# Differential attention: the low halves of the queries stored over all 128 partitions

## The chip, the cores and the metric

The kernel runs on one core of a Trainium2 chip. The metric is the device time of one execution in microseconds (us). TensorE (PE) multiplies matrices and transposes, VectorE (DVE) and ScalarE (ACT) do element-wise work, reductions and exponentials, GpSimd (POOL) does some of the casts and additions, and SyncE (SP) issues most transfers.

## The reference

The reference is a network of two layers over 512 latent and 256 context tokens of width 1024. Layer 0 mixes tokens with delta-rule and retention heads, layer 1 with differential softmax attention; each is followed by a layer norm, a gated feed-forward part with a 3x3 convolution, and another layer norm. Only layer 1's mixer matters here. It has 8 heads; each has two maps of queries and keys with 64 features and values with 128 features. The 512 latent queries read all 768 tokens:

```python
def diff_mix(q, k, v, lam):
    s = jnp.einsum('cbhqd,cbhkd->cbhqk', q, k).astype(jnp.float32) * DIFF_HD ** -0.5
    p = jax.nn.softmax(s, -1)
    a = p[0] - lam * p[1]
    return jnp.einsum('bhqk,bhkd->bhqd', a.astype(v.dtype), v)
...
    lp = lam_p.astype(f32)
    lam = jnp.exp(jnp.sum(lp[0] * lp[1])) - jnp.exp(jnp.sum(lp[2] * lp[3])) + lambda_init
```

After it come a root-mean-square norm per head and the output product with `w_out`. All is float32.

## The kernel before, in words

A float32 product is made of float32r (fp32r) products. Each operand is split into a high part (a rounding cast) and a low part (the rest), and three products are summed: high by high, high by low, low by high. Weights come in units: `unit` loads one (`raw`), ScalarE casts its high part `whi` (L147), and VectorE or GpSimd subtracts for the low part `wlo` (L148).

The program is written with a framework that orders the instructions of each engine by a priority, which is the place in the code plus an offset (`self.priority`). Each engine then runs its list in that fixed order and waits on semaphores.

`odd_mixer` (L1539) is the mixer of layer 1. It works on pairs of heads. `project` makes q, k and v of one pair, by pairs of token tiles: products `opj` of 256 columns (L115), the axial rotation `rope` (VectorE multiplies into `otok` and `ob`, L1574 and L1578; GpSimd adds, L1580), four transposes into `oT_ps` (L119), and then the evacuation with the split:

- `q_evac` (L1584) writes three tiles: the high part of map 0 on both halves of the partitions, the high part of map 1 likewise, and one tile with the low part of map 0 on partitions 0 to 63 and that of map 1 on 64 to 127. These are four ScalarE casts and two VectorE subtractions.
- `k_evac` writes for map 0 the high part on the lower and the low part on the upper partitions, and for map 1 the other way round.

`attend` handles one head, by four query tiles of 128 queries; 8 heads make 32 tiles. Per tile and map it fills a PSUM tile `sc` of 768 scores, by a piece of 512 and one of 256 columns. One product over all 128 rows gives high by high plus high by low (the query's high part is there twice). Two further products, over 64 rows each, add low by high. So a tile has four products over 128 rows and four over 64:

```python
for k0, n in ((0, 512), (512, 256)):
    for c, rows in enumerate((LO, HI)):
        self.mm(scs[c][:, k0:k0 + n], q[2][rows, i, t * P:(t + 1) * P], k[c][rows, i, k0:k0 + n],
                start=False)
```

Then VectorE takes the maximum `mx` (L1664) and scales it (L1665), ScalarE takes exponentials `pt` with their sum (L1667), VectorE forms the factor `nl` (L1671, L1672) and combines the two maps (L1675), TensorE transposes the result in six pieces (`aT_ps`, L119), ScalarE and VectorE copy them (L1683), and TensorE multiplies by the values (L115). VectorE copies the result into `oall` (L1687).

While heads of one pair are attended, the projection products of the next pair are emitted as filler, three steps per query tile, with a priority 100 later; so the scheduler puts `opj` products among the score products wherever these would wait. For the last pair the filler is the output product (`wo_ps`). The pools of the first steps, the constants `ca`, `sub`, `lp` and `nlam` among them, are opened before; `lp` and `l2` hold lambda's products.

Of the kernel before, what the change touches and what calls it, by code (L numbers as in the profile page):

```python
# [11 lines left out]
F32 = mybir.dt.float32  # L12
F32R = mybir.dt.float32r
I32 = mybir.dt.int32
AF = mybir.ActivationFunctionType
ALU = mybir.AluOpType
AX = mybir.AxisListType
# [3 lines left out]
P = 128  # L21
# [76 lines left out]
class Net:  # L98
# [22 lines left out]
    def rsqrt(self, pool, x, n, mul, add, tag):  # L121
        """(x*mul + add)^-0.5 on [128, n] float32, by three Newton steps (each flips the sign) to full precision."""
# [27 lines left out]
    def pin(self, ins):  # L150
        """Queue an instruction behind all that its engine was given so far."""
        return self.tc.keep_in_program_order(ins)

    @contextmanager
    def priority(self, offset):
        """Emit with a priority shifted by offset (positive: later)."""
# [9 lines left out]
    def hilo(self):  # L166
        """The two split halves of the next weight unit, from the open weight pools in turn."""
# [6 lines left out]
    def unit(self, parts, scale=None):  # L174
        """Load weight columns (list of [1024, w] DRAM blocks), scaled if asked for, and split them: [128, 8, 256]."""
# [14 lines left out]
    def unit_rows(self, src, scale=None):  # L190
        """Load [256, 1024] weight rows, with columns scaled if given, and split them: [128, 2, 1024]."""
# [10 lines left out]
    def proj_fm_g(self, w, c0, dsts):  # L202
        """Feature-major products: dsts = [(psum [128, n], t0, n)]; weights stationary."""
# [9 lines left out]
    def proj_tm_g(self, ps, w, t, c0=0, n=256):  # L213
        """Token-major products for token tile t; activations stationary."""
# [19 lines left out]
    def set_work(self, items, side=None):  # L234
        """items: [(weight parts, generator function of the loaded unit)], run in order by tick()."""
# [13 lines left out]
    def _step(self):  # L249
        """Advance the current item; its cost, or None at its end."""  # L250
# [19 lines left out]
    def drain(self, upto):  # L270
        """Run until the first `upto` items are complete."""
# [4 lines left out]
    def setup(self):  # L276
# [22 lines left out]
        self.cpad = cp.tile([P, KT, 32], F32, name="cpad")  # L299
        nc.gpsimd.memset(self.cpad, 0.0)  # L300
# [10 lines left out]
    def rows_T(self, pool, psp, src, n, dst, doff=0):  # L311
        """DRAM rows [n, 128] -> dst[:, doff:doff+n] (transposed)."""
# [7 lines left out]
    def cond(self, pool, psp):  # L320
        """silu(c), silu(c_ctx) as a zero-padded stationary operand [128, 8, 32]."""
# [22 lines left out]
    def mod_bias(self, pool, psp, l):  # L344
        """mod_b of layer l, per feature: [128, 48]."""
# [8 lines left out]
    def mod_group_g(self, mp, psp, l, g, tag="tr", bufs=2):  # L354
        """adaLN columns [2048 g, 2048 (g+1)) of layer l, both conditionings."""
# [30 lines left out]
    def h_params(self, key, lnidx, l, sub):  # L386
        """Scale/bias per feature of h = modulate(layer_norm(.)): from xhat."""
# [1426 lines left out]
```

## Time and profile before

| | us |
|---|---|
| runs | 2127.46, 2130.88, 2131.03 |
| median | 2130.88 |
| span of the profiled execution | 2123.7 |
| TensorE busy | 1976.3 (93%) |
| VectorE busy | 1297.5 (61%) |
| GpSimd busy | 789.0 (37%) |
| ScalarE busy | 703.5 (33%) |
| mean granted clock of TensorE | 0.971 |

The profile gives the profiled execution a span, from its first to its last instruction, of 2123.7 us, and no other time of its own; the three runs were 3.8 to 7.3 us above that span. The attention lies at about 1333 to 1670 us. In the rows below a line such as `PE L115 MATMUL sc<-ok,oq 64*128 64x512` reads: TensorE, line 115, product into the tile `sc` from `ok` and `oq`, 64 rows by 128 columns of the array, 512 columns streamed; `x6` counts like instructions in a run. A duration of TensorE overlaps the next one; the distance between starts is what an instruction takes of the engine. What stands in brackets is the time that the engine was idle before, and what ended it.

### The profile page before, as it was taken

The page shows a single profiled execution, that of the slowest core. Times are in us where ns is not written, and L with a number is a line of the kernel's source. Part 1 is how long each engine was busy: PE and PEld are TensorE (multiplying, and loading weights), DVE is VectorE, ACT ScalarE, POOL GpSimd, SP SyncE. Part 2 cuts the span into 40 slices and gives each one's busy share as a digit, 9 for nine tenths or more (in the row PEclk, how much of TensorE's full clock was granted, in tenths as well). Part 3 has the DMA queues.
Part 4 walks back from the last instruction along what each step waited for, and adds up shares of the span by engine and source line. Part 5 has one row for each costly group of instructions (what it writes and reads, how often), then busy time and mean ns, then how long its engine had stood idle before and what let it go on. Part 6 is the DMA issues. An engine that isn't in the chain of part 4 may idle for free. (4 is left out here: it accounts for less than half of the span.)

```text
span 2123.7 us, 33676 instructions
## 1 busy us (share of the span) xinstructions
PE 1976.3 (93%) x13766; PEld 1676.6 (79%) x13766; DVE 1297.5 (61%) x2570; ACT 703.5 (33%) x1228; POOL 789.0 (37%) x430
## 2 busy tenths in 40 slices
PE   6989999999998999999999988988997989999997
PEld 4777777778898988888888868878886987777776
DVE  2354745544358675665555584566567787767676
ACT  2331343523344422222222243444444453222221
POOL 1233222212422344444444442212023135756582
PEclk8999999999999999999999999999997999999999
DMA  8536335465623311111111112100103142223221
GB/s 255 166 121 181 109 119 149 126 182 168 180 80 120 124 65 60 60 60 60 60 60 60 60 60 68 41 29 32 41 31 100 50 139 100 99 80 99 80 80 40
DMA packets 195586, 201.34 MB, mean 95 GB/s; under 512 B 21112, under 2 KB 183512, under 8 KB 195432
## 3 DMA queue, kind: packets, MB, share of 16 engines
q1 hardware_dynamic: 194136, 197.57, 29.2%
q8 instruction: 108, 1.77, 0.3%
q10 hardware_dynamic: 1296, 1.62, 0.3%
q14 instruction: 46, 0.38, 0.1%
HBM read 185.89 MB, written 13.27 MB: 94 GB/s over the span
## 5 line engine op out<-in xcount | busy, mean ns | idle before, releaser
L148 POOL TENSOR_TENSOR wlo<-raw,whi 128x2048 fp32r<-128x2048 f32 (+2 forms) x154 | 416.7, 2730 | 533.6 <-ACT whi L147 509.4
L1442 DVE SCALAR_TENSOR_TENSOR ac<-g_ps,fconvT,ac 128x441 f32<-128x441 f32 (+2 forms) x352 | 244.4, 694 | 190.9 <-ACT ac L1431 180.9
L147 ACT CAST whi<-raw 128x2048 fp32r<-128x2048 f32 (+2 forms) x177 | 200.4, 1169 | 393.5 <-PE d_ps L115 180.9
L115 PE MATMUL d_ps<-whi,hh 128*128 128x512 f32 x440 | 177.8, 404 | 21.1 <-DVE gt L1391 20.0
L115 PE MATMUL d_ps<-whi,hl 128*128 128x512 f32 x440 | 172.8, 393 | 0.6 <-DVE hl L148 0.6
L115 PE MATMUL d_ps<-wlo,hh 128*128 128x512 f32 x440 | 172.9, 393 | 0.0
L1488 POOL TENSOR_TENSOR acc<-acc,gt 128x512 f32<-128x512 f32 x90 | 129.7, 1450 | 69.4 <-DVE gt L1391 69.4
L115 PE MATMUL opj<-whi,hTh 128*128 128x256 f32 x512 | 151.6, 296 | 1.1 <-ACT oq L1591 1.1
L1391 DVE TENSOR_TENSOR gt<-d_ps,gate 128x512 f32<-128x512 f32 x192 | 130.6, 684 | 31.1 <-PE d_ps L115 28.9
L115 PE MATMUL opj<-whi,hTl 128*128 128x256 f32 x512 | 148.1, 289 | 0.0
L115 PE MATMUL opj<-wlo,hTh 128*128 128x256 f32 x512 | 147.9, 289 | 0.0
L115 PE MATMUL g_ps<-hTl,whi 128*128 128x512 f32 (+1 forms) x384 | 144.7, 377 | 1.1 <-POOL hTl L148 1.1
L115 PE MATMUL u_ps<-hTl,whi 128*128 128x512 f32 (+1 forms) x384 | 144.8, 377 | 0.2
L115 PE MATMUL u_ps<-hTh,wlo 128*128 128x512 f32 (+1 forms) x384 | 144.6, 377 | 0.0
L115 PE MATMUL u_ps<-hTh,whi 128*128 128x512 f32 (+1 forms) x384 | 144.5, 377 | 0.0
L115 PE MATMUL g_ps<-hTh,whi 128*128 128x512 f32 (+1 forms) x384 | 144.4, 376 | 0.0
L115 PE MATMUL g_ps<-hTh,wlo 128*128 128x512 f32 (+1 forms) x384 | 144.2, 376 | 0.0
L115 PE MATMUL fpj<-whi,hTh 128*128 128x256 f32 x432 | 126.9, 294 | 5.8 <-DVE kT L550 4.7
L115 PE MATMUL fpj<-wlo,hTh 128*128 128x256 f32 x432 | 126.9, 294 | 0.0
L115 PEld LDWEIGHTS d_ps<-whi,hh 128*128 128x128 f32 x440 | 83.0, 189 | 55.2 <-DVE gt L1391 38.9
L115 PE MATMUL fpj<-whi,hTl 128*128 128x256 f32 x432 | 126.0, 292 | 0.0
L115 PEld LDWEIGHTS opj<-whi,hTh 128*128 128x128 f32 x512 | 98.8, 193 | 7.2 <-issue 4.4
(464 smaller groups left out, 5014.8 us busy)
## 6 DMA issues: line engine op xcount, KB each, us to landing
mraw<-in_mod_w_dram SPq DMA_DIRECT2D x80, 512.0 KB
raw<-in_f_w_gate_dram SPq DMA_DIRECT2D x22, 1024.0 KB
raw<-in_f_w_up_dram SPq DMA_DIRECT2D x22, 1024.0 KB
raw<-in_f_w_down_dram SPq DMA_DIRECT2D x22, 1024.0 KB
raw<-in_o_w_qkv_dram SPq DMA_DIRECT2D x12, 1024.0 KB
raw<-in_e_w_in_dram SPq DMA_DIRECT2D x10, 1024.0 KB
mraw<-in_mod_w_dram SPq DMA_DIRECT2D x32, 256.0 KB
raw<-in_e_w_in_dram SPq DMA_DIRECT2D x12, 512.0 KB
```

The costliest lines, as they stand in the source:

```text
L115: self.nc.tensor.matmul(out, lhsT=lhsT, rhs=rhs, start=start, stop=stop)
L147: self.nc.scalar.copy(h, r)
L148: lo_eng.tensor_sub(l, r, h.bitcast(F32))
L1391: v.tensor_mul(gt, ps, gates[0 if t < NLT else 1][:, n * 512:(n + 1) * 512])
L1442: v.scalar_tensor_tensor(out=o, in0=pv[:, r0 + di:r1 + di, c0 + dj:c1 + dj], scalar=cw[(di + 1) * 3 + dj + 1], in1=o, op0=ALU.mult, op1=AL ...
L1488: (v if n else g).tensor_add(o, o, gt)
```

## The change

The low part of each map's query is stored over both halves of the partitions, as the high part is; there are four query tiles instead of three. Every score product then runs over 128 rows, and low by low is added to the sum. The products come map by map: high 512, high 256, low 512, low 256 of map 0, then of map 1. `q_evac` has six ScalarE casts (two of them copy the low part from the one half to the other) and two VectorE subtractions.

Three more edits free memory for the fourth tile: the zero pad `cpad` moves from the pool of constants into a pool of layer 0's mixer, `lp` and `l2` into a pool `olp` of their own that is closed at once, and the rotation's `ob` has one buffer instead of two. The other lines of the diff take comments out.

```diff
-        self.cpad = cp.tile([P, KT, 32], F32, name="cpad")
-        nc.gpsimd.memset(self.cpad, 0.0)
...
     def even_mixer(self, accst):
         w_in = self.a["e_w_in"][0]
         with ExitStack() as outer:
             with ExitStack() as right:
                 p2 = self.pool(right, "d2", bufs=2, side="right")
+                self.cpad = p2.tile([P, KT, 32], F32, bufs=1, name="cpad")
+                self.nc.gpsimd.memset(self.cpad, 0.0)
...
-                lp = cpl.tile([P, 4, DH], F32, name="lp")
-                nc.scalar.dma_start(out=lp, in_=a["o_lambda"][0].partition_broadcast(P))
-                l2 = cpl.tile([P, 2], F32, name="l2")
-                for i in range(2):
-                    v.tensor_mul(lp[:, 2 * i], lp[:, 2 * i], lp[:, 2 * i + 1])
-                    v.reduce_sum(l2[:, i:i + 1], lp[:, 2 * i], axis=AX.X)
-                s_.activation(l2, l2, AF.Exp)
                 nlam = cpl.tile([P, 1], F32, name="nlam")
-                v.tensor_sub(nlam, l2[:, 1:2], l2[:, 0:1])
-                v.tensor_scalar_add(nlam, nlam, -LAMBDA_INIT)
+                with ExitStack() as tmp:
+                    lpp = self.pool(tmp, "olp")
+                    lp = lpp.tile([P, 4, DH], F32, name="lp")
+                    nc.scalar.dma_start(out=lp, in_=a["o_lambda"][0].partition_broadcast(P))
+                    l2 = lpp.tile([P, 2], F32, name="l2")
+                    for i in range(2):
+                        v.tensor_mul(lp[:, 2 * i], lp[:, 2 * i], lp[:, 2 * i + 1])
+                        v.reduce_sum(l2[:, i:i + 1], lp[:, 2 * i], axis=AX.X)
+                    s_.activation(l2, l2, AF.Exp)
+                    v.tensor_sub(nlam, l2[:, 1:2], l2[:, 0:1])
+                    v.tensor_scalar_add(nlam, nlam, -LAMBDA_INIT)
 
                 def rope(ps, t, out):
                     pv, ov = (x.rearrange("p (t h f n) -> p t h f n", t=2, h=4, f=2) for x in (ps, out))
-                    b = p2.tile([P, 2, 4, 2, 32], F32, tag="ob", name="ob")
+                    b = p2.tile([P, 2, 4, 2, 32], F32, tag="ob", bufs=1, name="ob")
                     v.tensor_mul(out.rearrange("p (t x n) -> p t x n", t=2, n=32),
                                  ps.rearrange("p (t x n) -> p t x n", t=2, n=32),
                                  cos[:, t:t + 2].unsqueeze(2).to_broadcast([P, 2, 8, 32]))
...
                 LO, HI = slice(0, DH), slice(DH, P)
 
                 def q_evac(q, ps, cs):
-                    s_.copy(q[0][LO, :, cs], ps[LO])
-                    s_.copy(q[1][HI, :, cs], ps[HI])
-                    v.tensor_sub(q[2][LO, :, cs], ps[LO], q[0][LO, :, cs].bitcast(F32))
-                    v.tensor_sub(q[2][HI, :, cs], ps[HI], q[1][HI, :, cs].bitcast(F32))
-                    s_.copy(q[0][HI, :, cs], ps[LO])
-                    s_.copy(q[1][LO, :, cs], ps[HI])
+                    for c, src in enumerate((ps[LO], ps[HI])):
+                        own, other = (LO, HI) if c == 0 else (HI, LO)
+                        s_.copy(q[c][own, :, cs], src)
+                        v.tensor_sub(q[2 + c][own, :, cs], src, q[c][own, :, cs].bitcast(F32))
+                        s_.copy(q[c][other, :, cs], src)
+                        s_.copy(q[2 + c][other, :, cs], q[2 + c][own, :, cs].bitcast(F32))
 
                 def k_evac(k, ps, cs):
                     s_.copy(k[0][LO, :, cs], ps[LO])
                     s_.copy(k[1][HI, :, cs], ps[HI])
                     v.tensor_sub(k[0][HI, :, cs], ps[LO], k[0][LO, :, cs].bitcast(F32))
                     v.tensor_sub(k[1][LO, :, cs], ps[HI], k[1][HI, :, cs].bitcast(F32))
 
                 def project(pr, passes, hd):
                     ws = self.next_units if pr == 0 else {}
                     hp = odd if pr % 2 else even
-                    hd["q"] = [hp.tile([P, 2, LAT], F32R, tag=f"oq{j}", name="oq") for j in range(3)]
+                    hd["q"] = [hp.tile([P, 2, LAT], F32R, tag=f"oq{j}", name="oq") for j in range(4)]
                     hd["k"] = [hp.tile([P, 2, TOK], F32R, tag=f"ok{j}", name="ok") for j in range(2)]
                     vt = hd["v"] = hp.tile([P, NT, 256], F32, tag="ov", name="ov")
                     pend = []
...
                                 yield
 
                 def attend(h, q, k, vt, i):
                     hc = slice(h * P, (h + 1) * P)
                     ss = pb.tile([P, NLT], F32, tag="oss", name="oss")
                     Zs = pb.tile([P, NLT, 2], F32, tag="oZ", name="oZ")
...
                         pr = []
                         scs = [scp.tile([P, 1024], F32, tag="sc", name="sc") for c in range(2)]
                         for c in range(2):
-                            for k0, n in ((0, 512), (512, 256)):
-                                self.mm(scs[c][:, k0:k0 + n], q[c][:, i, t * P:(t + 1) * P], k[c][:, i, k0:k0 + n],
-                                        stop=False)
-                        # the two maps' halves of the array work side by side
-                        for k0, n in ((0, 512), (512, 256)):
-                            for c, rows in enumerate((LO, HI)):
-                                self.mm(scs[c][:, k0:k0 + n], q[2][rows, i, t * P:(t + 1) * P], k[c][rows, i, k0:k0 + n],
-                                        start=False)
+                            for j in (0, 2):
+                                for k0, n in ((0, 512), (512, 256)):
+                                    self.mm(scs[c][:, k0:k0 + n], q[j + c][:, i, t * P:(t + 1) * P],
+                                            k[c][:, i, k0:k0 + n], start=(j == 0), stop=(j == 2))
```

The instructions are ordered anew. First TensorE, at a query tile of the second head of the first pair, with projections of the next pair between (`oq_12403` and `oq_12404` are the high tiles, `oq_12405` the low one). Before:

```order
L115 MATMUL sc_13674<-ok_12407,oq_12404 128x256
L115 MATMUL opj_13530<-wlo_13421,hTh_68 128x256
L115 MATMUL sc_13673<-ok_12406,oq_12405 128x512
L115 MATMUL opj_13530<-whi_13420,hTl_69 128x256
L115 MATMUL sc_13674<-ok_12407,oq_12405 128x512
L119 MATMUL aT_ps_13630<-ident_66,pt_13618 128x128 x4
L119 MATMUL aT_ps_13636<-ident_66,pt_13618 128x128 x2
L115 MATMUL opj_13530<-whi_13420,hTh_68 128x256
L115 MATMUL sc_13673<-ok_12406,oq_12405 128x256
L115 MATMUL opj_13530<-wlo_13421,hTh_68 128x256
L115 MATMUL sc_13674<-ok_12407,oq_12405 128x256
```

and with the change (`oq_12407` and `oq_12408` are the high tiles, `oq_12409` and `oq_12410` the low ones):

```order
L115 MATMUL opj_13544<-whi_13432,hTl_69 128x256
L115 MATMUL sc_13687<-ok_12411,oq_12409 128x512
L115 MATMUL opj_13544<-whi_13432,hTh_68 128x256
L115 MATMUL sc_13687<-ok_12411,oq_12409 128x256
L119 MATMUL aT_ps_13644<-ident_66,pt_13632 128x128 x4
L119 MATMUL aT_ps_13650<-ident_66,pt_13632 128x128 x2
L115 MATMUL opj_13544<-wlo_13433,hTh_68 128x256
L115 MATMUL sc_13688<-ok_12412,oq_12408 128x512
L115 MATMUL opj_13544<-whi_13432,hTl_69 128x256
L115 MATMUL sc_13688<-ok_12412,oq_12408 128x256
L115 MATMUL opj_13544<-whi_13432,hTh_68 128x256
L115 MATMUL sc_13688<-ok_12412,oq_12410 128x512
```

Map 0's four products now come first and together with their low part, and the transposes of the previous tile stand in front of map 1's.

Second ScalarE, at the first query evacuation of pair 1. Before:

```order
L1586 CAST oq<-oT_ps 64x2x256
L1587 CAST oq<-oT_ps 64x2x256
L1590 CAST oq<-oT_ps 64x2x256
L1591 CAST oq<-oT_ps 64x2x256
L147 CAST whi<-raw 128x2048
L1667 ACTIVATE pt,oZ<-sc,mx 128x768 x2
```

and with the change:

```order
L1590 CAST oq<-oT_ps 64x2x256
L1592 CAST oq<-oT_ps 64x2x256
L1593 CAST oq<-oq 64x2x256
L1590 CAST oq<-oT_ps 64x2x256
L147 CAST whi<-raw 128x2048
L1592 CAST oq<-oT_ps 64x2x256
L1593 CAST oq<-oq 64x2x256
L1665 ACTIVATE pt,oZ<-sc,mx 128x768 x2
```

The casts of the low part (L1593) stand between the others, a weight cast stands inside the evacuation, and the exponentials come after all of it.

Third TensorE again, at the first query evacuation of pair 1, whose transposes are `oT_ps`; `aT_ps<-ident,pt` are the transposes of the probabilities and `aT_ps<-ov,aT` the products with the values. Before:

```order
L115 MATMUL opj<-whi,hTl 128x256
L119 MATMUL oT_ps<-ident,otok 128x128 x4
L115 MATMUL opj<-whi,hTh 128x256
L115 MATMUL opj<-wlo,hTh 128x256
L119 MATMUL aT_ps<-ident,pt 128x128 x6
L115 MATMUL opj<-whi,hTl 128x256
L115 MATMUL opj<-whi,hTh 128x256
L115 MATMUL opj<-wlo,hTh 128x256
L115 MATMUL opj<-whi,hTl 128x256
L115 MATMUL opj<-whi,hTh 128x256
L115 MATMUL opj<-wlo,hTh 128x256
L115 MATMUL aT_ps<-ov,aT 128x128 x6
```

and with the change:

```order
L115 MATMUL opj<-whi,hTl 128x256
L119 MATMUL aT_ps<-ident,pt 128x128 x6
L119 MATMUL oT_ps<-ident,otok 128x128 x4
L115 MATMUL opj<-whi,hTh 128x256
L115 MATMUL aT_ps<-ov,aT 128x128 x6
L115 MATMUL opj<-wlo,hTh 128x256
L115 MATMUL opj<-whi,hTl 128x256
L115 MATMUL opj<-whi,hTh 128x256
```

The transposes of the probabilities went from two projections behind those of the queries to just ahead of them, and one projection instead of six stands ahead of the products with the values. At the second query evacuation of a pair the same transposes now stand 9 projections behind those of the queries, where 16, 16 and 20 stood in the three pairs, and their products 5 projections further on instead of 8. On VectorE, lambda's products and sums (L1566 and L1567 of the new code) now stand in the middle of the layer norm of the last token tile of layer 0; before they came behind the first key evacuation. In layer 0 the transfer of the retention heads' constants `cr`, `lg` and the exponentials of their masks stand later on ScalarE, and one `fo`, `fb` rotation later on VectorE.

## Rows read from the trace of the kernel before

**Rows 1.** Table of stretches: us, busy us of PE, PEld, DVE, ACT, POOL, clock, DMA, GB/s

```profile
1333.00:1600.00 267.00, 246.75 (x1784) 219.42 (x1782) 167.94 (x370) 113.07 (x224) 53.63 (x20) 0.97 0.11 36
...
1613.00:1640.00 27.00, 18.51 (x67) 14.25 (x66) 24.67 (x33) 9.40 (x15) 18.51 (x4) 0.50 0.29 97
```

**Rows 2.** Waits of TensorE, 1333 to 1600: total us, times, longest us

```profile
PE aT_ps L119 <- DVE pt L1675: 14.4, 10, 3.1
PE oT_ps L119 <- POOL otok L1580: 4.6, 6, 2.4
```

**Rows 3.** Waits of TensorE, 1600 to 1670

```profile
PE sc L115 <- ACT pt L1667: 6.2, 3, 3.2
```

**Rows 4.** Timeline of TensorE, an interleaved tile: start, us, instruction

```profile
1403.69 0.39 PE L115 MATMUL sc<-ok,oq 128*128 128x512 f32 x1
1403.92 0.28 PE L115 MATMUL opj<-whi,hTh 128*128 128x256 f32 x1
1404.04 0.28 PE L115 MATMUL sc<-ok,oq 128*128 128x256 f32 x1
1404.16 0.28 PE L115 MATMUL opj<-wlo,hTh 128*128 128x256 f32 x1
...
1404.80 0.39 PE L115 MATMUL opj<-whi,hTl 128*128 128x256 f32 x1
...
1405.54 0.88 PE L119 MATMUL aT_ps<-ident,pt 128*128 128x128 f32 x6
1406.17 0.36 PE L115 MATMUL opj<-whi,hTh 128*128 128x256 f32 x1
...
1406.78 0.39 PE L115 MATMUL opj<-wlo,hTh 128*128 128x256 f32 x1
...
1407.41 0.39 PE L115 MATMUL opj<-whi,hTl 128*128 128x256 f32 x1
```

**Rows 5.** Timeline of TensorE, a tile cut once

```profile
1364.58 1.30 PE L115 MATMUL sc<-ok,oq 128*128 128x512 f32 x6
...
1366.43 0.38 PE L115 MATMUL opj<-wlo,hTh 128*128 128x256 f32 x1
```

**Rows 6.** Timeline of TensorE, a tile in one piece

```profile
1379.45 1.49 PE L115 MATMUL sc<-ok,oq 128*128 128x512 f32 x8
1380.87 0.39 PE L115 MATMUL opj<-whi,hTh 128*128 128x256 f32 x1
```

**Rows 7.** Timeline of all engines, a hold in the attention

```profile
1387.72 4.54 POOL L148 TENSOR_TENSOR wlo<-raw,whi 128x2048 fp32r<-128x2048 f32 x1
...
1388.10 4.18 DVE L1672 SCALAR_TENSOR_TENSOR nl<-nl,oZ,nlam 128x1 f32<-128x1 f32 x1
...
1393.39 0.87 PE L119 MATMUL aT_ps<-ident,pt 128*128 128x128 f32 x6 [3.04 <-DVE pt L1675]
...
1394.02 0.37 PE L115 MATMUL opj<-wlo,hTh 128*128 128x256 f32 x1
...
1394.67 0.42 DVE L1683 COPY aT<-aT_ps 128x256 f32<-128x256 f32 x1
```

**Rows 8.** Instructions by form, 1270 to 1680: busy, mean ns, idle before, releaser

```profile
L1590 ACT CAST oq<-oT_ps 64x512 fp32r<-64x512 f32 x8 | 4.6, 577 | 9.6 <-DVE oq L1589 9.5
```

**Rows 9.** Timeline of GpSimd, an addition of the rotation

```profile
1386.49 1.28 POOL L1580 TENSOR_TENSOR otok<-otok,ob 128x512 f32<-128x512 f32 x1 [8.59 <-DVE ob L1578]
```

**Rows 10.** Instructions by form, 1270 to 1680, VectorE

```profile
L1558 DVE TENSOR_SCALAR sub<-sub 128x128 f32<-128x128 f32 x1 | 0.2, 227 | 1.5 <-DMA sub<-in_o_subln_w_dram 1.5
```

**Rows 11.** Timeline of VectorE, last layer norm of layer 0

```profile
1278.02 4.29 DVE L1230 SCALAR_TENSOR_TENSOR lns<-lny,lnh 128x1 f32<-128x1 f32 x1
```

**Rows 12.** Timeline of TensorE, first transposes of rotated tokens

```profile
1299.55 0.66 PE L119 MATMUL oT_ps<-ident,otok 128*128 128x128 f32 x4 [1.98 <-POOL otok L1580]
```

**Rows 13.** Waits of TensorE, 515 to 527

```profile
PE modt_ps L119 <- DVE modr L368: 3.0, 1, 3.0
```

**Rows 14.** Timeline of VectorE, last head pair

```profile
1615.99 4.47 DVE L136 SCALAR_TENSOR_TENSOR rs_y<-rs_w,rs_y 128x4 f32<-128x4 f32 x1
```

## The prediction

> **What bounds the kernel now.** The table of stretches comes first. In 1333 to 1600 us, where head pairs 0 to 2 are attended while the next pair is projected, TensorE is busy 246.75 of 267.00 us, VectorE 167.94, ScalarE 113.07 and GpSimd 53.63, at a granted clock of 0.97 [rows 1]. The list of TensorE's waits for the same stretch holds 14.4 us for VectorE's combined probabilities and 4.6 for GpSimd's rotated tokens, 19.0 together [rows 2], and 246.75 + 19.0 = 265.75 nearly fills the stretch. So TensorE's own steps set the time of these 24 query tiles, three quarters of the 32. The last pair is another matter: from 1613 to 1640 VectorE is busy 24.67 of 27 us, GpSimd 18.51, TensorE 18.51 too at a clock of 0.50 [rows 1]; TensorE waits there for ScalarE's exponentials [rows 3].
>
> The timeline of TensorE tells what a half-array product costs. The start of the next instruction is the honest step. Undisturbed, a projection product steps 0.12 us (1403.92 to 1404.04), a full 512-column score product 0.23 (1403.69 to 1403.92) and a full 256-column one 0.12 (1404.04 to 1404.16) [rows 4]. A half-array product (64 rows) between two full ones costs more: from 1404.16 to 1404.80 a projection and a half 512 take 0.64 where 0.35 is the undisturbed sum, +0.29; 1404.80 to 1405.54 takes 0.74, +0.39; 1406.17 to 1406.78, a projection and a half 256, takes 0.61 against 0.24, +0.37; 1406.78 to 1407.41 takes 0.63, +0.39 [rows 4]. That is 1.44 us for a tile whose four half products each stand alone. Eight of the 24 tiles are of this kind. Seven are cut in one or two places: one at 1364.58 takes 1.85 us to 1366.43 where four maps' worth of 0.35 and one projection of 0.12 would take 1.52, +0.33 [rows 5]; two cuts give up to twice 0.39. The rest run in one piece: eight score products from 1379.45 to 1380.87 take 1.42 us against 4 x 0.35 = 1.40 [rows 6].
>
> **The change, part by part.** *Full instead of half products.* Four half products per tile become four full ones with the same columns. In a tile of one piece, 1.42 becomes 1.40: nothing. In the eight fully interleaved tiles 1.4 us each goes, 11.2; in the seven cut ones about 0.5 each (between 0.33 and 0.78), 3.5. Sum -14.7 us, all on the engine that sets the time.
>
> The row says that two adjacent half products do not save anything here (1.42 against 1.40). The Trainium skill, TensorE: Matmul & The Clock Gate, in its table of small-K products, states that products sliced to distinct row groups run at the same time; by that a tile of one piece would take 3 x 0.35 = 1.05 us before, and the change would add 0.35 x 32 = 11.2 us. On the other side the Trainium skill, TensorEngine Tiling (Array Packing), Key Properties, says that a change of tiling mode drains TensorE; the extra 0.29 to 0.39 us agrees. The sum goes by the rows.
>
> *Transposes of the probabilities come sooner.* At the second query evacuation of pairs 0 to 2 the order puts the transposes 9 projection products behind those of the queries, where before 16, 16 and 20 stood between. At 1387.72 GpSimd casts a weight half for 4.54 us, VectorE's one-column instruction for the combination takes 4.18 us under it, and TensorE then stands 3.04 us [rows 7]. Fewer products in front mean a longer stand: (7 + 7 + 11) x 0.117 = +2.9 us. If the combination is ready sooner, because map 0's maximum no longer waits for the end of all eight products, it is 0; so 0 to +2.9, and I take +2.9, since the holder is GpSimd. The products that use these transposes follow 5 projections later instead of 8; at 1393.39 the copy of the second part into SBUF ended 1394.67 + 0.42 = 1395.09 [rows 7], 1.70 behind the start of the transposes, against 0.63 for the transposes themselves and 5 x 0.12 of projections, so 0.5 stays open where VectorE was held. 3 x 0.5 = +1.5, from 0 on where it was not. At the first query evacuation of each pair the transposes go ahead of those of the queries, and one projection instead of six stands between transposes and products: six projections were 0.70, now four query transposes (two thirds of 0.63) and one projection are 0.54, so 3 x 0.16 = +0.5.
>
> *Copies of the low half.* Each of 8 query evacuations gets two more casts on ScalarE of about 0.58 us [rows 8], 9.3 us in all. Map by map there are also two hand-overs to VectorE and back where there was one; the old third cast already waits for the subtraction, 9.5 us over eight [rows 8]. Behind them on ScalarE stand weight casts, the exponentials and the copies of the transposes. ScalarE is busy 113.07 of 267 us [rows 1] and so has 154 us in which to take 9.3; I put it at 0. Without that cover the second evacuation of each of three pairs, which the transposes follow, would hand its 2 x 0.58 on to TensorE: +3.5 at the other end.
>
> *The single buffer of the rotation.* VectorE's next rotation must now wait for GpSimd's addition of the last. That takes 1.28 us, and the next rotation comes 8.6 us later [rows 9]; even behind a 4.54 us weight cast [rows 7] it is done. 0, with +1 as an end.
>
> *Lambda's products* move on VectorE from behind the first key evacuation into the last layer norm of layer 0. Before they stood after a wait of 1.5 us for the transfer of the row in front of them [rows 10]; now they stand in the middle of the layer norm, where GpSimd holds a one-column instruction for 4.29 us [rows 11]; the hold may fall on one of theirs. If the transfer is late there, the norm is: +1.5, the wait seen. If VectorE is freer at the start of layer 1, TensorE's wait of 1.98 us for the first rotated tokens [rows 12] goes. Between -2.0 and +1.5; I take -0.5.
>
> *The zero pad and the order of layer 0.* The pad moves to another pool; a mask transfer and mask exponentials go behind a weight cast on ScalarE, and VectorE's rotation of one retention head behind a Newton chain; at this place TensorE waited 3.0 us for VectorE's copy of the modulation rows [rows 13]. The hold may fall on another instruction: that wait goes, or comes once more, -3 to +3; I take 0.
>
> *The last pair.* Here half products are cut too; at 0.72 us, half of 1.44, eight tiles hold 5.8 us. But VectorE and GpSimd set the time: a 4.47 us hold [rows 14] and the 6.2 us of waits for exponentials [rows 3] stay. Map 0's scores are done earlier, which starts its maximum earlier: I take -1.0, from -5.8 to +3.2 (one more of the waits of 3.2 [rows 3]).
>
> Sum: -14.7 + 2.9 + 1.5 + 0.5 - 0.5 - 1.0 = **-11.3 us**. The profiled span is 2123.7 us and the three runs read 2127.46 to 2131.03, median 2130.88, 7.2 above the span. So the span becomes 2112.4 and the time 2119.6, rounded to **2120 us**.
>
> **The rivals.** *Absorbed.* TensorE saves 14.7 us but runs into VectorE's combined probabilities, for which it already waited 14.4 us in ten places [rows 2]. If two thirds of the gain in the tiles with such waits turns into longer waits, 3 us is left: 2128. For it: the holds by GpSimd are fixed in length. Against it: those waits stand at ten of 24 tiles, and the fully cut tiles lie in stretches with projection products on both sides.
>
> *Slower: the copy chain on ScalarE.* The low copy is in order on ScalarE, behind a subtraction on VectorE, and VectorE is held up to 4.18 us by a GpSimd weight cast [rows 7]; the exponentials of the running tile are queued behind the copy. Six evacuations lie in the attention: 6 x 4.2 = 25 us, so 2120 + 25 = 2145. It decides from three of the six on (11.3 / 4.2). Against it: the third cast waited for the subtraction before too, and those waits sum to 9.5 us only [rows 8].
>
> *Slower: side by side after all.* Were adjacent halves overlapped, a tile of one piece would hold two full maps and one more, 3 x 0.35, and every tile now one 0.35 us longer: 32 x 0.35 = 11.2 us, 2142. The row of 1.42 us [rows 6] leaves little of it, unless a start costs what the overlap saves.
>
> *A larger gain.* The last pair gives its 5.8 instead of 1.0, and the earlier scores keep the 2.9 away: -11.3 - 4.8 - 2.9 = -19.0, 2112.
>
> *It does not do what it says.* If the cost at a cut belongs to the switch between score and projection products of any height, full products keep it: 2131. The full score products at 1403.69 and 1404.04 stand between projections without it [rows 4].
>
> **How the numbers follow.** Forecast 0.66; larger gain 0.07; absorbed 0.11; not what it says 0.04; copy chain 0.08; side by side 0.04. A measurement of this kernel can tell about 0.2%, 4.3 us, from no change. The forecast and the larger gain are faster by more than that, 0.73; absorbed and not what it says are within it, 0.15; the last two slower, 0.12. The range holds the first four cases: the last pair, layer 0 and the layer norm at their good ends take 4.8, 3.0 and 1.5 off, 9.3 in all, which gives 2110 from 2119.6; at the other end stands 2131, where nothing is left of the gain. Left out are the slower cases.
>
> **What would show it.** Right: in the timeline of TensorE no score product of 64 rows, a fully interleaved tile stepping 0.23 and 0.12 throughout, 1333 to 1600 shorter by about 9.8 us, the waits for combined probabilities at 14 to 20 us, and the rest of the program within 3 us of before. Wrong: a score product between projections that still steps 0.3 or more over its columns; waits of TensorE for ScalarE's casts or for probabilities above 25 us; tiles of one piece well under 1.40 us before, which would have shown as a loss; or a difference that lies in layer 0 or the feed-forward parts.

## The result and the profile after

The changed kernel takes 2112.89 us in the median of 16 runs, the kernel before 2123.69 us in the median of as many beside it. The ratio is 0.9945, with a 95% interval of 0.9931 to 0.9958: some 11.7 us faster by the ratio, 10.8 by the two medians. Measured again in two later sets it was 0.9949 (0.9931 to 0.9967) and 0.9943 (0.9929 to 0.9958). The forecast was 2120 from a median of 2130.88, a ratio of 0.9949.

The first profile after has a span of 2103.1 us, 20.6 less than that of before. That is too good by some 9 us: the profiled execution, 2104.85 us, is the fastest of the 16, which reach to 2122.93. Two further profiles of the same kernel have spans of 2110.4 and 2120.2. So stages are compared here over all three, each between the same two instructions of TensorE (the first product of one kind and the last of another):

| stage, us | before | changed, three profiles |
|---|---|---|
| start to first filler product of layer 0 | 130.8 | 127.7, 127.4, 129.5 |
| from there to the last norm of delta heads | 259.6 | 256.2, 255.3, 264.9 |
| from there to the output product of layer 0 | 258.5 | 261.2, 266.6, 263.4 |
| from there to the first projection of layer 1 | 620.0 | 620.1, 620.1, 620.0 |
| from there to the first score product | 64.5 | 59.9, 60.0, 60.0 |
| from there to the last projection (pairs 0 to 2) | 271.3 | 264.0, 266.1, 266.2 |
| from there to the last score product (pair 3) | 60.0 | 56.8, 57.2, 57.2 |
| from there to the end | 459.1 | 457.3, 457.7, 459.0 |

The first two lines vary between executions of one and the same kernel by up to 10 us and tell nothing. The three stages around the attention repeat within about 2 us.

First the table of stretches, for before and then for after, from the first score product to the last projection and on to the last score product (us, busy us of PE, PEld, DVE, ACT, POOL, clock, DMA share, GB/s):

```profile
1333.36:1604.62 271.26, 251.01 (x1818) 223.42 (x1816) 170.01 (x374) 115.22 (x230) 56.00 (x21) 0.97 0.11 36
1604.62:1664.66 60.04, 49.16 (x265) 38.44 (x264) 52.06 (x109) 28.81 (x60) 18.51 (x4) 0.77 0.24 79
```

```profile
1325.03:1589.00 263.97, 236.01 (x1818) 223.99 (x1817) 173.89 (x376) 123.80 (x243) 56.05 (x21) 0.97 0.11 37
1589.00:1645.80 56.80, 44.26 (x275) 38.46 (x274) 50.60 (x108) 28.52 (x57) 18.37 (x4) 0.82 0.26 84
```

TensorE does the same 1818 products in 236.01 us instead of 251.01: 15.0 us less. But the stretch is only 7.3 us shorter. Where the rest went stands in the list of TensorE's waits for that stretch, which answers to [rows 2]:

```profile
PE aT_ps L119 <- DVE pt L1673: 12.0, 11, 1.8
PE opj L115 <- DVE ob L1580: 8.0, 3, 2.9
PE aT_ps L115 <- DVE mx L1663: 6.9, 2, 3.4
PE sc L115 <- ACT oq L1592: 0.4, 1, 0.4
PE oT_ps L119 <- POOL otok L1582: 0.2, 1, 0.2
```

These are 27.5 us against 20.1 before, where the same stretch has the two lines of [rows 2] and this one:

```profile
PE opj L115 <- ACT oq L1591: 1.1, 3, 0.6
```

Two waits are new. Three times a projection waits for the rotation's reads on VectorE (8.0), and twice the products with the values wait 3.4 us for VectorE (6.9).

The timeline of TensorE at an interleaved tile answers to [rows 4]:

```profile
1402.69 0.28 PE L115 MATMUL opj<-wlo,hTh 128*128 128x256 f32 x1
1402.81 0.40 PE L115 MATMUL sc<-ok,oq 128*128 128x512 f32 x1
1403.04 0.28 PE L115 MATMUL opj<-whi,hTl 128*128 128x256 f32 x1
1403.16 0.28 PE L115 MATMUL sc<-ok,oq 128*128 128x256 f32 x1
1403.28 0.28 PE L115 MATMUL opj<-whi,hTh 128*128 128x256 f32 x1
```

The low products of map 0 (the one of 512 columns at 1402.81, the one of 256 at 1403.16) now step 0.23 and 0.12 us, and so do the projections around them, 0.12. The 0.29 to 0.39 us of each cut are gone. In a tile of one piece (against [rows 6]) nothing is gained:

```profile
1371.55 1.65 PE L115 MATMUL sc<-ok,oq 128*128 128x512 f32 x8
1373.04 0.28 PE L115 MATMUL opj<-whi,hTh 128*128 128x256 f32 x1
1373.15 0.28 PE L115 MATMUL opj<-wlo,hTh 128*128 128x256 f32 x1
```

The tile takes 1.49 us, where it took 1.42; the projection behind it steps 0.11 us. In the kernel before it stepped 0.23, from 1380.87 [rows 6] to the next one:

```profile
1381.10 0.28 PE L115 MATMUL opj<-wlo,hTh 128*128 128x256 f32 x1
```

Tile and projection together are 1.65 us before and 1.60 after, nearly the same.

### The profile page after: what moved, and what is told of

Its sections match the earlier page's. It is cut to its first block, busy times and chain, and to the rows that moved or that the text cites. A ratio compares the mean times of both kernels' runs of the same rounds, so it can differ in the third digit from the quotient of the medians.

```text
span 2103.1 us, 33680 instructions
## 1 busy us (share of the span) xinstructions
PE 1948.3 (93%) x13766; PEld 1671.1 (79%) x13766; DVE 1300.9 (62%) x2570; ACT 714.2 (34%) x1244; POOL 789.6 (38%) x430
## 3 DMA queue, kind: packets, MB, share of 16 engines
q8 instruction: 108, 1.77, 0.4%
```

## The experiments

Twelve runs were made, in three sets, each beside the kernel before: nine new kernels, one of them twice, and the changed kernel two more times. All but `memory_only` start from the changed kernel.

**The lows back on 64 rows, all else as changed** (`half_back`).

```diff
-for c in range(2):
-    for j in (0, 2):
-        for k0, n in ((0, 512), (512, 256)):
-            mm(scs[c][k0:k0+n], q[j + c], k[c])
+for c in range(2):
+    for k0, n in ((0, 512), (512, 256)):
+        mm(scs[c][k0:k0+n], q[c], k[c])
+for k0, n in ((0, 512), (512, 256)):
+    for c, rows in enumerate((LO, HI)):
+        mm(scs[c][k0:k0+n], q[2 + c][rows], k[c][rows])
```

> The changed kernel with its four low products per tile back on 64 rows each (low of map 0 on rows 0 to 63, low of map 1 on 64 to 127, in the old order: both highs, then 512 and 256 columns of the two maps alternately); evacuation and memory as changed; low by low is not added. Theory A (the switch of row height costs TensorE 0.3 to 0.4 us at each cut, and that is what the change saves): the stretch from the first score product to the last projection is 271 us again instead of 264, and the kernel is 7 to 12 us slower than the changed one, within 0.2% of before or up to 4 us faster. Theory B (the gain comes from the memory edits and the new order of layer 0 and of the start): the time stays 8 to 12 us under before. Theory C (the gain comes from the order map by map, which starts map 0's maximum earlier): back at before too, but then full products in this same order must be back as well.

Measured: 0.9985 (0.9971 to 0.9998), 2123.13 us against 2127.26. The stretch of pairs 0 to 2 is 271.4 us. Theory A, as expected: most of the gain is gone.

**Full products in the old order** (`full_old_order`). As above, but with `q[2 + c]` and `k[c]` over all rows.

> The changed kernel with full products in the old order (both maps' highs, then the lows by 512 and 256 columns alternately). Its order on TensorE is the same as that of the kernel with 64-row lows in this call, so the two differ in the height of the lows alone. Theory A: 7 to 12 us faster than that one, 0.4 to 0.6% faster than before, stretch from the first score product to the last projection 264 us give or take 3. Theory C (order map by map): no faster than the kernel with 64-row lows, within 0.2% of before. Theory B: both alike, 8 to 12 us under before.

Measured: 0.9947 (0.9928 to 0.9967), 2115.42 us; the stretch is 261.8 us, that of pair 3 is 57.3 against 60.1. This kernel and the last have the same order on TensorE and differ in the height of 128 products alone; between them lie 7.7 us of the medians and 12.4 us (331.5 to 319.1) from the first to the last score product in the two profiles. The intervals do not overlap. The height makes the gain; the order map by map is not needed (theory C falls), and the other edits do not make it (theory B falls). About 3 us of the 11.7 are not covered by this pair: `half_back`, which has all the other edits, is 0.15% ahead of before.

**The two halves of the rows, grouped** (`half_grouped`). As `half_back`, with the loop over maps outside that over columns.

> 64-row lows again, but grouped: 512 and 256 columns of map 0 (rows 0 to 63), then 512 and 256 of map 1 (rows 64 to 127). It tells whether adjacent products on the two halves of the rows run side by side. If they do, and the switch of height costs what this saves (theory A, second form): an uninterrupted tile of eight products takes 0.70 + 0.58 + 0.37 = 1.65 us instead of 1.42, and the kernel is 2 to 6 us slower than the one with alternating lows. If they do not overlap at all (the reading in the prediction): 1.42 us again, and the two kernels alike within 2 us.

Measured: 0.9997 (0.9980 to 1.0013). A tile of one piece takes 1.43 us:

```profile
1376.43 1.50 PE L115 MATMUL sc<-ok,oq 128*128 128x512 f32 x8
1377.86 0.39 PE L115 MATMUL opj<-whi,hTh 128*128 128x256 f32 x1
```

By what was written ahead this speaks for no overlap, but it does not: in the trace the two products of 512 columns start 0.007 us apart here too (1377.308 and 1377.315), though one of 256 stands between them in the order and starts only at 1377.645. My expectation of 1.65 us took for granted that products on different rows start in turn. In the medians the kernel is 3.5 us slower than `half_back`, inside the 2 to 6 us that were forecast for overlap, but the intervals overlap. It did not tell the two readings apart.

**All lows on the same rows** (`half_same_rows`). As `half_back`, but both maps read rows 0 to 63; the term low by high of map 1 is left out.

```diff
-        mm(scs[c][k0:k0+n], q[2 + c][rows], k[c][rows])
+        mm(scs[c][k0:k0+n], q[2 + c][LO], k[c][LO])
```

> The kernel with 64-row lows and alternating maps, but map 1's low product reads rows 0 to 63 too (low by low instead of low by high of map 1, whose term is left out), so that all four low products of a tile lie on the same rows and none has a neighbour on the other rows. If neighbours on different rows run side by side: an uninterrupted tile takes 0.70 + 0.70 + 0.37 = 1.77 us against 1.42, a pair between projections 0.12 to 0.23 more, and the kernel is 4 to 9 us slower than the one with lows on both halves. If they do not overlap: 1.42 us, and the two kernels alike within 2 us.

Measured: 0.9988 (0.9971 to 1.0005), no slower than `half_back`. But the tile of one piece, in the timeline of `half_back` and then of this kernel, shows what was asked:

```profile
1380.78 1.50 PE L115 MATMUL sc<-ok,oq 128*128 128x512 f32 x8
1382.21 0.39 PE L115 MATMUL opj<-whi,hTh 128*128 128x256 f32 x1
```

```profile
1378.97 1.83 PE L115 MATMUL sc<-ok,oq 128*128 128x512 f32 x8
1380.74 0.38 PE L115 MATMUL opj<-whi,hTh 128*128 128x256 f32 x1
```

1.43 us with the lows on both halves, 1.77 with all on one, as forecast for products that run side by side. So adjacent halves do overlap. They save 0.34 us per tile, and the change of height, in and out, costs about 0.37: one half product with one projection takes 0.61 us in [rows 4], and in [rows 5] two halves with one projection take 0.63, where 0.24 would be plain for one product and one projection of 256 columns. The rows of the second case:

```profile
1365.80 0.38 PE L115 MATMUL opj<-whi,hTh 128*128 128x256 f32 x1
1366.12 0.38 PE L115 MATMUL sc<-ok,oq 64*128 64x256 f32 x2
1366.43 0.38 PE L115 MATMUL opj<-wlo,hTh 128*128 128x256 f32 x1
```

The 1.42 of [rows 6] was a saving and a price that cancel. The trace of the kernel before had it already: inside the one row `x8` of [rows 6] the two half products of 512 columns start at 1380.327 and 1380.331, and the two of 256 at 1380.664 and 1380.666. A row that merges eight instructions hides that.

Why then is the kernel not slower? Its table of stretches beside that of `half_back`, from the first score product to the last projection, `half_back` first:

```profile
1334.29:1605.68 271.39, 253.84 (x1817) 225.54 (x1816) 168.00 (x375) 122.63 (x243) 56.07 (x21) 0.97 0.11 36
```

```profile
1332.40:1601.80 269.40, 250.75 (x1817) 221.72 (x1816) 166.86 (x375) 122.60 (x243) 56.07 (x21) 1.00 0.11 36
```

The clock column is 1.00 here and 0.97 there. `half_back` has five pieces of 3.4 us at the lower level in this stretch, this kernel none. At half speed five pieces cost up to 5 x 1.7 = 8.5 us of work, more than the low products gained in length (about 5 us by the busy times: 250.75 - 253.84 + 8.5, an estimate). That explains these two executions. Over all twelve runs of each kernel the mean granted clocks are closer, 0.9703 and 0.9716, which is worth some 3 us of 2123; the 2 to 3 us that are left lie within the intervals. The whole time was the wrong place to look; the tile's rows were the right one.

**The memory edits alone, on the kernel before** (`memory_only`).

```diff
-        self.cpad = cp.tile([P, KT, 32], F32, name="cpad")
...
+                self.cpad = p2.tile([P, KT, 32], F32, bufs=1, name="cpad")
...
+                    lpp = self.pool(tmp, "olp")
...
+                    b = p2.tile([P, 2, 4, 2, 32], F32, tag="ob", bufs=1, name="ob")
```

> The kernel before with the three memory edits alone (zero pad in the pool of layer 0, lambda's products in a pool of their own, one buffer for the rotation's second half); three query tiles and 64-row lows as before. Theory A: within 0.2% of before; the start of layer 1 (first projection to first score product) 3 to 4.6 us shorter, as in all four kernels with these edits, layer 0 between 390 and 650 us some 3 to 6 us longer. Theory B: 5 us or more faster than before in the median.

Measured: 0.9985 (0.9969 to 1.0001): 3 us by the ratio, not told from zero, and the same ratio as `half_back`. So some 3 of the 11.7 us may belong to these edits; that is not shown. The start of layer 1 is 1.8 us shorter, less than expected; in the twelve profiles of kernels with four query tiles that stage is 3.2 to 5.4 us shorter.

**The evacuation in the old grouping** (`evac_grouped`).

```diff
-for c, src in enumerate((ps[LO], ps[HI])):
-    copy(q[c][own], src); sub(q[2 + c][own], src, q[c][own])
-    copy(q[c][other], src); copy(q[2 + c][other], q[2 + c][own])
+copy(q[0][LO], ps[LO]); copy(q[1][HI], ps[HI])
+sub(q[2][LO], ps[LO], q[0][LO]); sub(q[3][HI], ps[HI], q[1][HI])
+copy(q[0][HI], ps[LO]); copy(q[1][LO], ps[HI])
+copy(q[2][HI], q[2][LO]); copy(q[3][LO], q[3][HI])
```

> The changed kernel with the query evacuation in the old grouping: both own casts, both subtractions, both other casts, then the two copies of the low halves. In the changed kernel TensorE waits three times 2.9 us, 8.0 in all, for the rotation's reads of a projection (VectorE), behind the second subtraction of an evacuation done map by map. If the map-by-map hand-overs make that wait: it goes to under 3 us, and the kernel is 3 to 6 us faster than the changed one. If the single buffer of the rotation makes it: 8 us again, and no change within 0.2%.

Measured: 0.9961 (0.9945 to 0.9978), no gain, and its list of waits for the stretch (1335 to 1603):

```profile
PE aT_ps L119 <- DVE pt L1675: 17.3, 13, 3.1
PE aT_ps L115 <- DVE mx L1665: 6.9, 2, 3.5
PE oT_ps L119 <- POOL otok L1582: 1.6, 3, 0.5
PE opj L115 <- ACT oq L1593: 1.3, 3, 0.6
PE sc L115 <- ACT oq L1593: 0.3, 1, 0.3
```

The 8.0 us of waits for the rotation are gone, so the hand-overs map by map made them and the single buffer did not. But the waits for combined probabilities went from 12.0 to 17.3. The time was handed on, not saved.

**Old order and old grouping together** (`full_old_order_evac`, run twice).

> Full products in the old order, with the evacuation in the old grouping: both changes together, to see whether a version beats the changed kernel. Theory A: the stretch from the first to the last score product, 320.8 and 323.3 us in the changed kernel and 319.1 with the old order, falls to 313 to 318; the ratio to before 0.991 to 0.995. If VectorE's holds take up the gain: 0.995 again.

Measured: 0.9931 (0.9912 to 0.9949); from the first to the last score product it takes 317.8 us, at the upper end of what was expected. The second time, beside the changed kernel:

> Full products in the old order with the evacuation in the old grouping once more, beside the changed kernel in the same call, to see whether it beats it: the intervals so far are 0.9912 to 0.9949 against 0.9931 to 0.9967. Ratio 0.992 to 0.994 if it does, 0.995 if that was chance.

0.9920 (0.9904 to 0.9936) against the changed kernel's 0.9943 (0.9929 to 0.9958) in the same set: lower both times, by 0.1 to 0.2%, but the intervals overlap; probably better, not shown.

**The casts in quarters** (`changed_cast_quarters`, and with the last two edits `best_cast_quarters`). What the saved time ran into can be seen in the changed kernel's timeline of all engines at the second of the new waits:

```profile
1416.20 4.52 POOL L148 TENSOR_TENSOR wlo<-raw,whi 128x2048 fp32r<-128x2048 f32 x1 [31.78 <-ACT whi L147]
...
1416.82 3.92 DVE L1691 TENSOR_TENSOR oss<-oss,orz 128x4 f32<-128x4 f32 x1
1420.66 0.41 DVE L1681 COPY aT<-aT_ps 128x256 f32<-128x256 f32 x1
...
1421.22 1.72 PE L115 MATMUL aT_ps<-ov,aT 128*128 128x128 f32 x12 [3.45 <-DVE mx L1663]
```

A four-column product on VectorE takes 3.92 us while GpSimd casts, the copy behind it is late, and TensorE stands 3.45 us. (The view names VectorE's `mx`, the last before; it is the copy at 1420.66 that these products read.) The same instruction takes 0.15 us at 1595.02, where GpSimd stands idle. The Trainium skill, SBUF — State Buffer, Who interferes with whom, says that the pair of ports that VectorE and GpSimd share is an exclusive lock, held for a whole instruction; the row agrees, since the instruction ends within 0.1 us of the cast. The edit shortens the instruction that holds it:

```diff
+        keep, self.cparts = self.cparts, 4 if pr else self.cparts
-        return {k: self.unit([w[...]]) for k in kinds}
+        r = {k: self.unit([w[...]]) for k in kinds}
+        self.cparts = keep
+        return r
```

> The changed kernel with the weight casts of the projections of pairs 1 to 3 (high on ScalarE, low on GpSimd) in four quarters instead of one piece. Theory D (what the saved product time ran into is VectorE held by GpSimd's 4.5 us casts, and the drops of TensorE's clock behind those waits): no one-column VectorE instruction of the attention takes over 1.5 us, TensorE's waits from the first score product to the last projection, 27 to 32 us in the two profiles of the changed kernel, fall below 20, at most two drops of the clock instead of four, and the kernel is 5 to 12 us faster than the changed one. Rival: VectorE waits for its own chain, and the holds only fill time that is lost anyway; then under 3 us.

Measured: 0.9890 (0.9872 to 0.9909), 2105.76 us, 10.2 us under the changed kernel's 2115.93 in the same set:

> The changed kernel unaltered, as the measure for the other three: ratio to before 0.994 to 0.995.

The details of the expectation, against the third profile of the changed kernel: TensorE's listed waits fell from 27.4 to 19.3 us, and the distances of over 0.75 us between two starts from 29.9 to 20.1, just not below 20. The list of waits of this kernel:

```profile
PE aT_ps L119 <- DVE pt L1676: 8.2, 12, 1.5
PE aT_ps L119 <- DVE rs_w L135: 4.0, 2, 2.0
PE opj L115 <- ACT oq L1595: 2.9, 2, 1.5
PE opj L115 <- DVE ob L1583: 2.6, 1, 2.6
PE oT_ps L119 <- POOL otok L1585: 1.2, 3, 0.4
PE sc L115 <- ACT oq L1595: 0.4, 1, 0.4
```

The two waits of 3.5 us are gone; the projections behind the query evacuations still wait 5.5 us (the two lines `opj`), where it was 8.1. Up to the last projection no one-column or four-column VectorE instruction takes over 1.3 us. In the last pair, where GpSimd works on blocks of `w_out` that were not cut, one of four columns still takes 4.46 us. Drops of the clock in the stretch went from six pieces of 3.4 us to two. The stretch in the table, the third profile of the changed kernel and then this one:

```profile
1337.90:1604.10 266.20, 238.52 (x1818) 226.99 (x1817) 174.06 (x376) 123.69 (x243) 56.01 (x21) 0.96 0.11 37
```

```profile
1332.40:1585.20 252.80, 233.27 (x1817) 221.26 (x1816) 164.27 (x376) 125.86 (x267) 62.96 (x45) 0.99 0.12 39
```

13.4 us less. VectorE's factor `nl` shows it too, by form, first in the changed kernel (first profile), then here:

```profile
L1670 DVE SCALAR_TENSOR_TENSOR nl<-nl,oZ,nlam 128x1 f32<-128x1 f32 x24 | 16.6, 692 | 0.6
```

```profile
L1673 DVE SCALAR_TENSOR_TENSOR nl<-nl,oZ,nlam 128x1 f32<-128x1 f32 x23 | 6.5, 281 | 0.6
```

The forecast of theory D came, and so did its sign in VectorE's rows. But the edit cuts ScalarE's casts as well as GpSimd's, and the two were not separated. With the old order and the old grouping:

> Full products in the old order, evacuation in the old grouping, and the casts in quarters. Theory D: 2100 to 2107 us where before has 2127, ratio 0.987 to 0.991. Rival: 0.992 to 0.994 as without the quarters.

Measured: 0.9848 (0.9826 to 0.9870), 2092.46 us, better than was forecast. This version beats both kernels; its stretch is 247.5 us, and TensorE is busy in 234.18 of them at a clock of 0.99. Whether the quarters would have helped the kernel before as much was not tried.

**The changed kernel again** (`changed_again`).

> The changed kernel once more, unaltered, for a second profile. Its first profile is 3.1 us ahead of before by 130 us into the program and 6.5 us at 360 us, where the change does nothing but move the zero pad. Theory A: that is variation of transfers between executions; here the lead by 130 us lies anywhere from -3 to +4 us and the time at 0.9945 of before. Theory B: 3 us at 130 us and 6 us at 360 us again.

Measured: 0.9949 (0.9931 to 0.9967). The lead by 130 us was 3.4 us again, and 1.3 us in the third profile; the kernels with the same memory edits lie between 3.8 us ahead (`memory_only`) and 2.4 us behind (`full_old_order_evac`). So it varies with the execution.

## Why the prediction was right, and where its terms were off

**Full instead of half products**, forecast at -14.7 us: TensorE's busy time in the stretch fell by 15.0. The size is right (12.5 in the third profile, where two more pieces at the low clock cost up to 3.4). The mechanism behind "nothing" for a tile of one piece was read wrongly: the step said that two adjacent halves save nothing. They do run side by side (1.77 us without, 1.43 with), and a change of height costs what they save. The rule of packed products in the Trainium skill, TensorE: Matmul & The Clock Gate, Why this matters for your kernels, which the sum set aside, holds in this trace: the halves start 0.003 us apart in the tile of `half_back`. The loss that was worked out from it does not come, since the change of height goes along with the overlap, and a half product between full ones pays the whole of that price.

**The transposes that come sooner and the products behind them**, forecast at +4.9 together: the waits of the stretch rose from 20.1 to 27.5 us as listed, and the distances of over 0.75 us between two starts from 20.9 to 29.9. The terms were short by 2.5 to 4 us, and the waiting stands elsewhere: the waits of the transposes themselves fell from 14.4 to 12.0, the products behind them wait 6.9 where 1.5 was forecast, and 8.0 come at a place whose terms were put at 0. What failed is the step that **put the copies of the low half at 0** because ScalarE had room. Their busy time was indeed covered, but the hand-overs map by map hold VectorE's second subtraction, then the rotation behind it, then the projection that needs the rotation's PSUM tile: 8.0 us. Around the first of the three VectorE is busy nearly throughout and GpSimd does nothing (columns as above):

```profile
1375.00:1378.10 3.10, 0.99 (x9) 0.80 (x7) 3.01 (x8) 2.81 (x3) 0.00 (x0) 1.00 0.01 3
```

At the other two it is the same: VectorE is busy 2.37 of 2.60 us and 2.81 of 2.90, GpSimd not at all. So the 8.0 us come of VectorE's own order of work, in which two maxima stand ahead of the second subtraction, and the 6.9 us of VectorE held by GpSimd. `evac_grouped` took the 8.0 away, and about as much came back, most of it as waits for probabilities. The rival of the absorbed gain was half right: 7 to 9 of 15 us went into waits.

**The single buffer of the rotation**, 0: right, by the same experiment.

**Lambda's products and the start of layer 1**, forecast at -0.5 between -2.0 and +1.5: the stage is 4.5 us shorter in all three profiles, beyond the range. In the waits of that stage the layer norm's 2.9 us became 1.5, and those for the first rotated tokens 2.9 became 0.8 (against [rows 12]): 3.5 of the 4.5. `memory_only` has 1.8 us of it; what makes the rest was not taken apart.

**Layer 0**, 0 with 3 either way: from the last norm of the delta heads to the output product 2.7 to 8.1 us longer in the three profiles, 1.4 to 8.1 in all thirteen profiles with the moved pad. TensorE's wait for the modulation rows went from 3.0 to 3.4 [rows 13] in all three; most of the rest lies in many small steps and is open.

**The last pair**, -1.0: -2.8 to -3.2. TensorE's busy time fell there by 4.9 us in the first profile, against the 5.8 that two cuts per tile gave. The clock rose from 0.77 to 0.82 in this stage too; what part of the 4.9 us that makes was not taken apart.

That the sum of -11.3 met -11.7 is luck in part: its terms were off in both directions, with too little waiting, and too little gain in the last pair and at the start of layer 1. For the stretch of pairs 0 to 2 alone -9.8 was forecast, and the three profiles have -7.3, -5.2 and -5.1. Of the signs named ahead, the tile's steps came; the waits for combined probabilities (12.0, not 14 to 20) and the rest of the program (not within 3 us, by the start of layer 1 and layer 0) did not. The slower rivals did not come.

## What to carry to other kernels

In this kernel a product on half of the rows gained nothing: right beside its partner it saved as much as the change of height cost, and alone between full products it cost 0.3 to 0.4 us. Where a scheduler mixes such products with full ones, try to fill the other half, even with superfluous rows. A saving on the busiest engine is worth what the next wait leaves of it: here 5 to 7 of 15 us, until the weight casts were cut in four. And where the median varies more than the effect, decide by the rows of the tile that the question is about.

## What the runs showed of the hardware that was not expected

- Products on different halves of the rows start within 0.01 us of each other, even when a product for the first half stands between them in the order (`half_grouped`).
- The clock of TensorE falls from 2.4 to 1.2 GHz for 3.4 us, at times for 6.8, behind some of its waits. In the changed kernel TensorE stood idle for 2.59 us up to 1378.58, and from 1378.1 the clock is low; it stood 3.45 us up to 1421.22, and the same came from 1422.5:

```profile
1378.10:1381.50 3.40, 2.92 (x14) 2.95 (x15) 0.50 (x3) 3.13 (x7) 2.90 (x2) 0.51 0.00 0
1417.00:1422.50 5.50, 2.05 (x18) 1.88 (x17) 5.47 (x9) 1.44 (x4) 3.72 (x1) 1.00 0.08 18
1422.50:1425.90 3.40, 3.40 (x18) 3.40 (x17) 2.96 (x16) 1.19 (x4) 0.00 (x0) 0.50 0.83 285
```

Each such piece costs up to 1.7 us of work beside the wait itself, half of 3.4 (an estimate). Before had four in the stretch, the changed kernel four to six, `half_same_rows` none and `best_cast_quarters` one. The length of a wait alone does not decide it: in `half_back` the clock fell behind waits of 1.86 to 2.81 us, and in `half_same_rows` seven waits of 1.86 to 2.49 us passed without a drop. The prediction had no term for it.
